# A decoder layer on one core: later closing of gates, other places for the attention values' products, earlier loads of the branches, and another order at the seam to the up-projection

## The chip, the cores and the metric

The kernel runs on one core of a Trainium2 chip. The time is that of the device, in microseconds, for one execution of the whole program. The engines are named as in the profile: PE multiplies matrices, ACT and DVE work on what lies in memory or in PE's accumulation banks, POOL works on memory only, SP issues transfers. Each engine works through its own queue in order and waits at an instruction until what that needs is there.

## The reference

One layer of a hybrid decoder, 1024 tokens of width 1024, all in float32:

```
h    = rms_norm(x);  P = h @ w_in                 # columns for all branches and their gates
y_a  = RWKV-7 mixing (8 heads x 64, state recurrence over the tokens, group norm)
y_b  = stick-breaking attention (8 heads x 64)
y_m  = cross-attention to 256 memory tokens (4 heads x 128)
merged = sum_b sigmoid(G_b) * (y_b @ w_branch[b])
x    = x + merged @ w_out
x    = x + (silu(gate) * val) @ w_down,  gate, val = conv3(rms_norm(x) @ w_up)
```

The result has to agree in float32. Most products are therefore done as three: each operand is split into a high half that PE takes at full rate and the rest, and high by high, high by low and low by high are summed.

## The kernel before, in words

Everything runs in one program whose order is written out by generators: an outer one (preparation of the recurrence, the two attentions, the recurrence itself) is woven with a filler, the projections and gates of later branches, which `yield` after each group of six matmuls. So a step of the outer work that is moved by one `yield` moves past one such group on PE (1.36 us, six matmuls), and instructions marked as pinned keep the order in which they were written on their engine. Within an engine nothing overtakes.

- **Preparation** (`rwkv_prep`, four head pairs). `shifted` takes a finished projection from its bank (L248), scales a shifted copy on ACT (L249) and adds both on DVE (L251). `chain` makes, per pair and half, the products bk (L381) and r times P (L382 to L384) from which `gram` multiplies on PE; `turned` has eight transposes and takes their result out of the bank on DVE at L398.
- **Stick-breaking attention** (`sb_attn`, 64 units). `front(u)` multiplies queries by keys and takes a sigmoid on ACT; `weigh(u)` is a scan on DVE (L838); `mid(u)` transposes the weights on PE and takes them out on ACT (L850); `back(u)` multiplies them by the values, for two units at a time, 32 times in all. The filler beside it are the gates of the branches (`gate_item`); a finished gate is closed by `close_gates` within the next gate (DVE L740, ACT L743, and a transfer).
- **Memory attention** (`mem_attn`, 8 units) has the same shape: scores, row maximum and Exp (DVE L1050, ACT L1053), transposes, values. Its queries come from `mem_q`, whose product is split at L1015 (ACT) and L1017 (DVE).
- **Recurrence and branches** (`stage2`, `branch`). The recurrence takes small products out of banks on ACT (L549, L561). For a branch `load_y` loads four tiles into buffers of tag `w4` and splits them: ACT L1101 for the high half, DVE L1102 for the low half. `norm_quarter` ends with a reciprocal root: `rsqrt` issues L168 on DVE and a power on POOL (L169), and L593 on DVE multiplies by it.
- **Output projection and seam** (`out_proj`, `up_phase`). Each of eight row tiles is multiplied, added to x (L1230), squared (L1231), normed (L1233, L168, L169, L1235), transposed (`spread`) and, as operand of a block scheme with seven products instead of eight, summed (L1261 to L1266) and split (L1271 on ACT, L1272 on DVE or POOL). In `up_phase` `prep1` to `prep3` provide the split weights (L1351, L1354) and `step(n, i)` issues product i of column pair n; L1448 takes the first product out of its bank.

The up and down products that follow run on PE from 1250 us to the end.

Of the kernel before, what the change touches and what calls it, by code (L numbers as in the profile page):

```python
# [49 lines left out]
class Trunk:  # L50
# [120 lines left out]
    def startup(self):  # L171
# [41 lines left out]
        self.wa = self.shifted(12, "A", pps[0])  # L213
        nc.scalar.activation(self.wa[0:64], self.wa[0:64], AF.Tanh)
        self.sg = self.shifted(13, "A", pps[1])
        nc.scalar.activation(self.sg, self.sg, AF.Sigmoid)
        return self.shifted(4, "at", pps[2])
# [24 lines left out]
    def shifted(self, ti, tag, pp=None):  # L242
# [7 lines left out]
        out = self.t4(tag)  # L250
        nc.vector.scalar_tensor_tensor(out, pr, self.omm[:, ti : ti + 1], tmp, ALU.mult, ALU.add)  # L251
        return out
# [35 lines left out]
    def shift_item(self, ti, out, name):  # L288
# [10 lines left out]
        out.append(self.shifted(ti, "at", pp))  # L299
        self.fresh.append(name)  # L300
        yield
# [5 lines left out]
    def rwkv_prep(self, p, krv, need):  # L307
# [66 lines left out]
        def chain(h):  # L374
            hs = halves[h]
            bk, ra = self.t4("qk"), self.t4("qk")
            bk4, ra4 = (x.rearrange("p (c u s) -> p c u s", c=8, u=2) for x in (bk, ra))
            for x, first in ((b, 1), (kp, 0)):
                for h2 in range(2):
                    q = slice(h2 * 64, h2 * 64 + 64)  # L380
                    nc.vector.tensor_tensor(bk4[q, :, first ^ h2], self.c8(x[q, hs]), self.c8(Q[q, hs]), ALU.mult)  # L381
            nc.vector.tensor_tensor(ra4[:, :, 0], self.c8(r[:, hs]), self.c8(P[:, hs]), ALU.mult)  # L382
            nc.vector.scalar_tensor_tensor(ra4[:, :, 1, 1:64], self.c8(P[:, hs])[:, :, 0:63], -1.0, self.c8(kk[:, hs])[:, :, 1:64], ALU.mult, ALU.mult)
            nc.vector.tensor_scalar(ra4[:, :, 1, 0], self.c8(kk[:, hs])[:, :, 0], -math.exp(OFF), None, ALU.mult)  # L384
# [188 lines left out]
    def norm_quarter(self, i, junk):  # L573
# [17 lines left out]
        yield  # L591
# [102 lines left out]
    def proj_item(self, src, fin, hook={}):  # L694
# [119 lines left out]
    def sb_attn(self, qk, need):  # L814
# [80 lines left out]
    def mem_kv(self):  # L895
# [18 lines left out]
        def ss():  # L914
            pst = self.ps("g")
            for j in range(2):
                for k in range(8):
                    o = (k % 4) * 256 + j * 128
                    self.colsum(pst[:, j : j + 1], sqs[k // 4][:, o : o + 128], self.ones[:, 0:1], k == 0, k == 7)
# [86 lines left out]
    def mem_q(self, h, out, hook):  # L1006
# [3 lines left out]
        def fin(pp):  # L1010
            sq = self.t4()
            qhi, qlo = self.t4("qk", F32R), self.t4("qk", F32R)
            for i in range(2):
                hs = slice(i * 512, (i + 1) * 512)
                nc.scalar.activation(qhi[:, hs], pp[i], AF.Copy, scale=self.par("memq"))  # L1015
                nc.scalar.activation(sq[:, hs], pp[i], AF.Square)
                nc.vector.scalar_tensor_tensor(qlo[:, hs], pp[i], self.par("memq"), qhi[:, hs].bitcast(F32), ALU.mult, ALU.subtract)  # L1017
# [11 lines left out]
    def mem_attn(self, mq, need):  # L1029
# [51 lines left out]
        for s in range(len(units) + 4):  # L1081
            if s >= 4:
                back(s - 4)
            if s < len(units):
                front(s)
            yield
            if 2 <= s < len(units) + 2:
                mid(s - 2)
# [56 lines left out]
    def branch(self, b, first):  # L1145
        st = {}

        def load():
            st["y"] = self.load_y(b)
# [6 lines left out]
        return load, items  # L1156
# [43 lines left out]
    def out_proj(self):  # L1200
# [21 lines left out]
        def norm(tt, pp):  # L1222
            x = self.t4()
# [4 lines left out]
            for n in range(2):  # L1228
                ns = slice(n * 512, (n + 1) * 512)
                nc.vector.tensor_tensor(x[:, ns], pp[n], x[:, ns], ALU.add)  # L1230
                nc.scalar.activation(sq[:, ns], x[:, ns], AF.Square, accum_out=ss[:, n : n + 1])  # L1231
            nc.scalar.dma_start(self.x2d[tt], x)
            nc.vector.tensor_tensor(rs, ss[:, 0:1], ss[:, 1:2], ALU.add)  # L1233
            self.rsqrt(rs, rs, 1, 1.0 / D, 1e-6)
            nc.scalar.activation(sq, x, AF.Copy, scale=rs)  # L1235
            return sq

        def spread(tt, sq):
            tl = slice((tt % 4) * 128, (tt % 4 + 1) * 128)
            for kb in range(2):  # L1240
# [4 lines left out]
                for kk in range(4):  # L1245
# [3 lines left out]
                    if kk < 2:  # L1249
                        nc.scalar.activation(dst, src, AF.Copy, scale=self.par("g2", k))  # L1250
# [604 lines left out]
```

## Time and profile before

| | |
|---|---|
| median of three runs | 1858.47 us (1855.64 to 1860.42) |
| the profiled execution, its own time | 1856.43 us |
| its span, first to last instruction | 1854.7 us |
| PE busy | 1796.9 us, 97% |
| DVE, ACT, POOL busy | 63%, 47%, 43% |
| mean granted clock of PE | 0.991 |

The span is what the rows of the trace add up to; the profiled execution's own time lies 1.73 us above it and the median 2.04 us above that. In rows of the timeline the columns are start, duration, engine, line, operation, operands, shape and count; in square brackets stands how long the engine idled just before and whom it waited for. A row of waits has the total, the number and the longest. In rows of windows each engine's busy time is followed by its number of instructions, and PEclk is the granted clock.

### The profile page before, as it was taken

What the parts mean: (1) busy time and instruction counts of PE and PEld (TensorE: products, weight loads), DVE (VectorE), ACT (ScalarE), POOL (GpSimd) and SP (SyncE); (2) the same over time, 40 slices, a digit from 0 to 9 for tenths busy, and PEclk for the clock granted to TensorE, in tenths of its full rate; (3) what the DMA queues carried; (4) which work ended last, traced back from release to release, by engine and by line L of the source; (5) the groups of instructions that cost most, each with busy time, mean ns of one, the idle gap of its engine ahead of it and who ended that gap; (6) DMA issues with size and microseconds to landing.
All of it is one profiled execution on the core that took longest, in us unless ns stands there. A gap on an engine that the chain in (4) does not pass through costs nothing. (4 is left out here: it accounts for less than half of the span.)

```text
span 1854.7 us, 27269 instructions
## 1 busy us (share of the span) xinstructions
PE 1796.9 (97%) x10468; PEld 1451.4 (78%) x10468; DVE 1170.1 (63%) x1623; ACT 866.7 (47%) x1553; POOL 788.6 (43%) x447
## 2 busy tenths in 40 slices
PE   8999999999999999998999999979999999999999
PEld 6777778778787887776777878768888888878877
DVE  5657664998887514334333882467776777785595
ACT  5443343565565635533443443454454444444433
POOL 2322343222221452122322541487776767545454
PEclk9999999999999999999999999999999999999999
DMA  4155465111112441568654462323232233395475
GB/s 180 58 170 182 158 201 187 49 43 64 40 52 78 112 128 40 177 237 281 229 171 161 163 235 102 114 68 109 95 124 88 97 114 108 120 326 203 141 247 185
DMA packets 122339, 261.28 MB, mean 141 GB/s; under 512 B 28505, under 2 KB 43097, under 8 KB 122082
## 3 DMA queue, kind: packets, MB, share of 16 engines
q1 hardware_dynamic: 84738, 193.71, 32.2%
q10 hardware_dynamic: 33696, 53.23, 7.9%
q0 software_dynamic: 3776, 12.62, 2.2%
q8 instruction: 82, 1.34, 0.3%
q14 instruction: 47, 0.39, 0.1%
HBM read 178.99 MB, written 80.48 MB: 140 GB/s over the span
## 5 line engine op out<-in xcount | busy, mean ns | idle before, releaser
L81 POOL TENSOR_TENSOR wl<-wr,wh 128x1024 fp32r<-128x1024 f32 x77 | 195.0, 2533 | 479.8 <-ACT wh L80 479.8
L112 PE MATMUL mm<-xhi,wh 128*128 128x512 f32 x784 | 266.0, 420 | 9.1 <-ACT xhi L182 7.4
L112 PE MATMUL mm<-xlo,wh 128*128 128x512 f32 x784 | 247.2, 397 | 0.7 <-DVE xlo L183 0.7
L112 PE MATMUL mm<-xhi,wl 128*128 128x512 f32 x784 | 244.4, 393 | 0.0
L112 PEld LDWEIGHTS mm<-xlo,wh 128*128 128x128 f32 x784 | 149.5, 191 | 35.1 <-DVE xlo L183 1.5
L112 PEld LDWEIGHTS mm<-xhi,wl 128*128 128x128 f32 x784 | 148.9, 190 | 33.8 <-POOL wl L81 0.5
L112 PEld LDWEIGHTS mm<-xhi,wh 128*128 128x128 f32 x784 | 138.5, 192 | 39.8 <-issue 9.1
L80 ACT ACTIVATE wh<-wr 128x1024 fp32r<-128x1024 f32 x77 | 81.5, 1059 | 153.8 <-PE mm L112 89.6
L112 PE MATMUL mm<-dw,da 128*128 128x512 f32 x528 | 121.3, 390 | 1.5 <-DVE da L1593 1.4
L112 PE MATMUL mm<-BT,l 128*128 128x512 f32 x504 | 117.9, 389 | 1.0 <-POOL l L1354 1.0
L112 PEld LDWEIGHTS mm<-dw,da 128*128 128x128 f32 x528 | 98.9, 188 | 23.3 <-DVE da L1593 2.3
L1594 POOL TENSOR_TENSOR dw<-draw,dw 128x512 fp32r<-128x512 f32 x55 | 80.5, 1471 | 84.9 <-ACT dw L1592 82.2
L112 PE MATMUL mm<-BT,wh 128*128 128x512 f32 x352 | 109.8, 393 | 3.2 <-DVE u L1406 3.2
L838 DVE TENSOR_TENSOR_SCAN at<-at,nrt 128x128 f32<-128x128 f32 (+3 forms) x64 | 91.2, 1428 | 32.3 <-ACT at L832 32.2
L112 PEld LDWEIGHTS mm<-BT,l 128*128 128x128 f32 x504 | 94.5, 188 | 21.0 <-POOL l L1354 1.4
L112 PE MATMUL mm<-B,wh 128*128 128x512 f32 x352 | 108.5, 389 | 2.1 <-ACT p L1448 2.1
L1593 DVE TENSOR_TENSOR da<-draw,da 128x512 fp32r<-128x512 f32 x77 | 67.0, 878 | 60.3 <-ACT da L1591 59.7
L112 PE MATMUL g<-dw,da 128*128 128x512 f32 x396 | 92.4, 394 | 2.2 <-ACT dw L1592 1.1
L1354 POOL TENSOR_TENSOR l<-it,l 128x1024 fp32r<-128x1024 f32 x21 | 50.8, 2421 | 94.4 <-ACT l L1351 94.4
L112 PEld LDWEIGHTS g<-dw,da 128*128 128x128 f32 x396 | 75.4, 191 | 18.7 <-ACT dw L1592 1.6
L1591 ACT ACTIVATE da<-draw 128x512 fp32r<-128x512 f32 x77 | 48.3, 629 | 84.3 <-PE mm L112 41.0
L169 POOL TENSOR_TENSOR hf<-rs,half 128x16 f32<-128x16 f32 (+1 forms) x17 | 48.5, 2856 | 86.1 <-DVE rs L168 85.7
(329 smaller groups left out, 3982.2 us busy)
## 6 DMA issues: line engine op xcount, KB each, us to landing
wr<-in_w_in_dram SPq DMA_DIRECT2D x50, 512.0 KB, 3.6
draw<-actd SPq DMA_DIRECT2D x77, 256.0 KB, 3.4
draw<-in_w_down_dram SPq DMA_DIRECT2D x55, 256.0 KB, 4.6
at<-scr SPq DMA_DIRECT2D x24, 512.0 KB, 6.2
wr<-in_w_up_dram SPq DMA_DIRECT2D x22, 512.0 KB, 3.5
actd<-gall ACTq DMA_DIRECT2D x44, 256.0 KB, 3.3
rw<-in_w_up_dram SPq DMA_DIRECT2D x20, 512.0 KB, 3.9
gsd<-w ACTq DMA_DIRECT2D x18, 512.0 KB, 2.7
```

The lines of the kernel that those rows point to most:

```text
L80: self.nc.scalar.activation(hi, raw, AF.Copy)
L81: self.nc.gpsimd.tensor_tensor(lo, raw, hi.bitcast(F32), ALU.subtract)
L112: self.pinned(self.nc.tensor.matmul(*a, **k))
L169: nc.gpsimd.tensor_tensor(out, t[:, :n], self.half[:, :n], ALU.pow)
L838: self.pinned(nc.vector.tensor_tensor_scan(sn[:, :W][:, ::-1], sn[:, :W][:, ::-1], self.nrt[:, 1152 - W :][:, ::-1], 1.0, ALU.mult, ALU.max))
L1354: nc.gpsimd.tensor_tensor(lo, src, hi.bitcast(F32), ALU.subtract)
L1591: self.pinned(nc.scalar.activation(A[:, 0], a, AF.Copy))
L1593: self.pinned(nc.vector.tensor_tensor(A[:, 1], a, A[:, 0].bitcast(F32), ALU.subtract))
L1594: nc.gpsimd.tensor_tensor(Wt[:, 1], w, Wt[:, 0].bitcast(F32), ALU.subtract)
```

## The change

It keeps the arithmetic and the number of matmuls and moves work:

- in the preparation r times P stands ahead of the bk products in `chain`; the last addition of `shifted` is issued one `yield` later; `turned(0)` comes one `yield` later and `gram(1, 0)` stays;
- in both attentions `front` comes first, then a `yield`, then `back`, directly ahead of the transposes of `mid`; gates are closed at the fifth group of the next gate instead of the third; `spread_last` is hooked into a gate;
- the two halves of the memory queries' split are pinned, and the norm sums of the memory keys are in two parts;
- a branch's y is loaded into the buffers of tag `A`, in which the low half then stays, and is split piece by piece in a gate that lies ahead of the branch;
- `norm_quarter` goes on three `yield`s after the root instead of one;
- in `out_proj` the four POOL splits of two operands are done two and two, the second two behind the norm of tile 4; in `up_phase` the norm of tile 7, the sums, the high and the low splits are written in another order, the first products have a bank each and are taken out at once, and the products of the first pair come in the order 5, 6, 7, 4, 3 instead of 6, 5, 7, 4, 3.

```diff
-        out.append(self.shifted(ti, "at", pp))
+        rest = self.shifted(ti, "at", pp)
+        yield
+        out.append(rest())
         self.fresh.append(name)
-        yield
...
         u1 = chain(1)
-        for _ in range(2):
+        for _ in range(3):
             yield
         turned(0, bp)
         bp = decayed(1, u1[0])
-        for _ in range(4):
+        for _ in range(3):
             yield
         gram(1, 0, *u1)
...
         self.rsqrt(rs, vs, 16, 1.0 / 64, 64e-5)
-        yield
+        for _ in range(3):
+            yield
...
-            if k == 2:
+            if k == 4:
                 self.close_gates()
...
         for u in range(len(units) + 4):
+            if u < len(units):
+                front(u)
             if u % 2 == 0:
+                yield
                 if u >= 4:
                     back(u - 4)
-                if u < len(units):
-                    front(u)
-                yield
-            elif u < len(units):
-                front(u)
             if 2 <= u < len(units) + 2:
                 mid(u - 2)
...
-                nc.vector.scalar_tensor_tensor(qlo[:, hs], pp[i], self.par("memq"), qhi[:, hs].bitcast(F32), ALU.mult, ALU.subtract)
+                self.pinned(nc.vector.scalar_tensor_tensor(qlo[:, hs], pp[i], self.par("memq"), qhi[:, hs].bitcast(F32), ALU.mult, ALU.subtract))
...
     def load_y(self, b):
-        ys = []
+        hi = self.pool_a.tile([128, 4, 1024], F32R, name=self.nm("yhi"), tag="inst")
+        los = [self.t4("A", F32R) for _ in range(4)]
         for k in range(4):
-            y = self.t4("w4")
-            self.nc.sync.dma_start(y, self.yd[b, k])
-            ys.append(y)
-        return self.split_y(ys)
+            self.nc.sync.dma_start(los[k].bitcast(F32), self.yd[b, k])
+
+        def part(k):
+            y = los[k].bitcast(F32)
+            self.pinned(self.nc.scalar.activation(hi[:, k], y, AF.Copy))
+            self.pinned(self.nc.vector.tensor_tensor(los[k], y, hi[:, k].bitcast(F32), ALU.subtract))
...
+        def side(i):
+            name, src = ("11", "21")[i], [halves(j)[i] for j in range(2)]
+            operand(name, self.pool_l, "l4")
+            split_hi(name, src)
+            split_lo(name, src, nc.gpsimd)
...
+            drain(norm(tt, pp))
+            if tt == 4:
+                side(1)
...
+        hi("22", old)
+        hi("T1", old, (0,))
+        hi("T2", old)
+        next(norm)
+        lo("T1", old, (0,))
+        next(norm)
+        hi("T1", old, (1,))
+        lo("T2", old)
+        lo("22", old, eng=nc.gpsimd)
         step(0, 1)
-        step(1, 1)
-        late(7)
...
+        evacuate(0)
+        next(norm, None)
+        st[1, "A"] = bank()
+        product(1, 1, st[1, "A"], True, True)
+        spread()
+        evacuate(1)
...
-        items += [lambda: drain(inv), ld1, gate(), gate(), mark("y1"), *br1, ld2, gate(), *br2, gate()]
+        items += [lambda: drain(inv), gate(), ld1, gate(hk1), mark("y1"), *br1, ld2, gate(hk2), *br2, gate()]
```

**ACT, the load of branch 2 within the recurrence**, before (w is the tile that y was loaded into, yhi the high half, qk the recurrence's matrices taken out of banks g):

```order
L80 ACTIVATE wh_7571<-wr_7569 128x1024
L1101 ACTIVATE yhi_7556<-w_1310_7548 128x1024
L549 ACTIVATE qk_7234<-g_7469 64x64 x2
L549 ACTIVATE qk_7234<-g_7470 64x64
L1101 ACTIVATE yhi_7556<-w_1311_7550 128x1024
L549 ACTIVATE qk_7234<-g_7470 64x64
L549 ACTIVATE qk_7239<-g_7471 64x64 x2
L549 ACTIVATE qk_7239<-g_7472 64x64 x2
L561 ACTIVATE qk_6779<-g_7469 64x64 x2
```

and now (L1121 is the former L1101, L554 the former L549, L566 the former L561):

```order
L80 ACTIVATE wh_7555<-wr_7553 128x1024
L554 ACTIVATE qk_7230<-g_7465 64x64 x2
L554 ACTIVATE qk_7230<-g_7466 64x64 x2
L554 ACTIVATE qk_7235<-g_7467 64x64 x2
L554 ACTIVATE qk_7235<-g_7468 64x64 x2
L1121 ACTIVATE yhi_7544<-A_7545 128x1024
L1121 ACTIVATE yhi_7544<-A_7546 128x1024
L566 ACTIVATE qk_6764<-g_7465 64x64 x2
```

The splits no longer stand within the eight L549 but behind them, and ahead of the eight L561.

**POOL, output projection**, before (B are the low halves of two operands, ss the root of tile 4's norm):

```order
L1272 TENSOR_TENSOR B_1_1_10238<-raw_9862,B_0_1_10236 128x1024
L1272 TENSOR_TENSOR B_1_0_10245<-raw_9862,B_0_0_10243 128x1024
L1272 TENSOR_TENSOR B_1_1_10246<-raw_9862,B_0_1_10244 128x1024
L169 TENSOR_TENSOR ss_1616_10272<-rs_10279,half 128x1
L1303 TENSOR_TENSOR wsum_10352<-wsec_10351 128x512
```

and now:

```order
L1292 TENSOR_TENSOR B_1_1_10230<-raw_9854,B_0_1_10228 128x1024
L169 TENSOR_TENSOR ss_1608_10256<-rs_10263,half 128x1
L1292 TENSOR_TENSOR B_1_0_10269<-raw_9854,B_0_0_10267 128x1024
L1292 TENSOR_TENSOR B_1_1_10270<-raw_9854,B_0_1_10268 128x1024
L1327 TENSOR_TENSOR wsum_10344<-wsec_10343 128x512
```

Two of the four splits have gone behind the root.

**ACT, the seam**, before (p takes the first product out of its bank, sq is tile 7's norm, BT and B high halves):

```order
L1231 ACTIVATE sq_10549,ss_1646_10551<-w_1645_10548 128x512 x2
L1235 ACTIVATE sq_10549<-w_1645_10548,ss_1646_10551 128x1024
L1271 ACTIVATE BT_0_0_10567<-t_1575_9867 128x2x384
L1271 ACTIVATE B_0_0_10579<-A_9865 128x2x384
L1271 ACTIVATE BT_0_1_10568<-t_1576_9868 128x2x384
L1271 ACTIVATE B_0_1_10580<-A_9866 128x2x384
L1448 ACTIVATE p_1649_10605<-mm_10592 128x512
L1448 ACTIVATE p_1651_10620<-mm_10607 128x512
```

and now:

```order
L1244 ACTIVATE sq_10568,ss_1638_10570<-x_1637_10567 128x512 x2
L1287 ACTIVATE BT_0_1_10550<-raw_9854 128x2x384
L1473 ACTIVATE p_1641_10599<-mm_10586 128x512
L1250 ACTIVATE sq_10568<-x_1637_10567,ss_1638_10570 128x1024
L1265 ACTIVATE A_9855<-g_10615,params 128x128 x2
L1265 ACTIVATE A_9857<-g_10624,params 128x128 x2
L1473 ACTIVATE p_1645_10633<-mm_10602 128x512
```

The first product is taken out ahead of the norm's last step, and the splits that stood between have gone ahead of the squares.

More of the change, by code (lines that the diff above doesn't have):

```diff
@@ L1086, in mem_attn @@
             yield
+            if s >= 4:
+                back(s - 4)
             if 2 <= s < len(units) + 2:
@@ L1268, in split @@
-        def split(name, src, eng, ts=slice(0, 512)):
-            for j in range(2):
+            sub = lambda o, x, y: self.pinned(nc.vector.tensor_tensor(o, x, y, ALU.subtract))
+            for half in which:
+                for j in range(2):
+                    b11, b21, b12, b22 = (x[:, :, ts] for x in halves(j))
+                    if half == 0:
+                        sub(b11, b12, b11)
+                        sub(t2[j][:, :, ts], b22, b11)
+                    else:
+                        sub(b12, b22, b12)
+                        sub(b21, t2[j][:, :, ts], b21)
@@ L1311, in out_proj @@
         w1 = weights(0, "at")
+        drain = lambda g: [None for _ in g]
         for tt in range(2):
-            sqs[tt] = norm(tt, first[tt])
+            drain(norm(tt, first[tt]))
         for tt in range(2, 8):
@@ L1499, in u1_first @@
             nc.scalar.activation(u[:, L2], A, AF.Copy)
-        def parts(name, eng):
-            for ts in (old, new):
-                split(name, src[name], eng, ts)
+        hi = lambda name, ts=slice(0, 512), js=(0, 1): split_hi(name, src[name], ts, js)
+        lo = lambda name, ts=slice(0, 512), js=(0, 1), eng=nc.vector: split_lo(name, src[name], eng, ts, js)
         self.pin = True
```

160 lines of the change are left out of this document (90 added, 70 removed).

## The prediction

> **What bounds the kernel now.** I read the page first, then the chain of waits, the waits of PE, and around each of them the timeline of the engine that PE waited for.
>
> ```profile
> PE 1796.9 (97%) x10468; PEld 1451.4 (78%) x10468; DVE 1170.1 (63%) x1623; ACT 866.7 (47%) x1553; POOL 788.6 (43%) x447
> 1250.28 381.40 PE mm L112 x1680
> 1250.00:1640.00 390.00, 389.72 (x1718) 322.40 (x1719) 292.37 (x438) 182.70 (x252) 271.19 (x158) 1.00 0.34 113
> ```
>
> PE is the bound: in the long up phase the chain is one piece of 1680 matmuls, and 1718 in 390 us make 0.227 us each. The change adds no matmul, and whatever is saved ahead of 1250 us moves all that follows. At most 1854.7 - 1796.9 = 57.8 us of idle PE can be won, plus lost clock.
>
> ```profile
> PE g L105 <- DVE at L398: 6.4, 3, 2.6
> PE g L112 <- ACT qk L549: 6.0, 1, 6.0
> PE g L105 <- ACT at L850: 3.7, 2, 2.8
> PE g L112 <- ACT at L1053: 2.8, 1, 2.8
> 1226.50:1229.90 3.40, 3.40 (x10) 2.64 (x9) 0.00 (x0) 0.21 (x2) 3.32 (x4) 0.50 0.00 0
> 1230.00:1233.40 3.40, 3.40 (x17) 2.77 (x16) 1.92 (x3) 2.49 (x3) 3.40 (x3) 1.00 0.39 106
> ```
>
> The idle is a few single waits. The last two rows show a second loss: 3.4 us at half clock after an idle, with 10 matmuls where the next 3.4 us hold 17. Half of 3.4 us, 1.7 us, is lost each time. By the granted clock in such rows, the idles at 103, 496, 718, 873 (two windows), 985 and 1171 us are followed by such a window; those at 217 and 272 are not.
>
> **The change, part by part.** *Preparation.*
>
> ```profile
> 103.52 1.92 PE L105 MATMUL g<-kon,it 128*128 128x128 f32 x8 [2.23 <-DVE at L398]
> 216.63 1.16 PE L105 MATMUL g<-kon,it 128*128 128x128 f32 x8 [1.62 <-DVE at L398]
> 272.25 1.25 PE L105 MATMUL g<-kon,it 128*128 128x128 f32 x8 [2.57 <-DVE at L398]
> 101.48 1.28 DVE L251 SCALAR_TENSOR_TENSOR at<-w,omm,w 128x1024 f32<-128x1024 f32 x1 [1.21 <-ACT w L249]
> 102.69 2.48 DVE L398 TENSOR_TENSOR at<-g,kon 128x512 f32<-128x512 f32 x4
> 153.47 1.16 PE L112 MATMUL g<-qk,qk 64*128 64x128 f32 x16 [1.68 <-DVE qk L384]
> 153.24 2.79 DVE L381 TENSOR_TENSOR qk<-qk,qk 64x512 f32<-64x512 f32 x4
> ```
>
> The transposes wait for banks that L398 empties; L398 stands behind L251, which waits 1.21 us for ACT and takes 1.28. Now L251 is issued one group later, behind L398, and the transposes too come 1.36 us later: 1.21 + 1.28 + 1.36 = 3.85 us, more than the longest of the three waits. They go: 2.23 + 1.62 + 2.57 and one window of 1.7, 8.1 us. Against it, the grams at 153 and 208 need the last bk product, which now ends the row of products on DVE where the short L384 did: one of four L381, 0.70 us, each. That makes 6.7.
>
> *Stick-breaking attention.*
>
> ```profile
> 495.99 1.07 PE L105 MATMUL g<-kon,at 128*128 128x128 f32 x4 [2.78 <-ACT at L850]
> 494.39 1.06 ACT L743 ACTIVATE w<-w 128x1024 f32<-128x1024 f32 x1 [4.99 <-DVE w L740]
> sum 300.00, PE 291.79 PEld 237.40 DVE 252.57 ACT 171.25 POOL 77.48; mean PE 48.63 PEld 39.57 DVE 42.09 ACT 28.54 POOL 12.91
> ```
>
> ACT stood 4.99 us at the closing of a gate, with L850 behind it. Closed two groups later (2.7 us and the attention's work between them), the closing finds L740 done: 2.78 + 1.7 = 4.5. For the values' products themselves I take nothing: the same matmuls are issued, their operands two units old. What their new neighbours cost is bounded, either way, by 32 x 0.12 = 3.8 us: the pair of matmuls at 1209.70 (below), first of its kind after others, takes 0.73 where a pair in a row takes 0.61. DVE is busy 252.57 of 300 us here (the sum of six windows from 300 to 600 us), so waits for it can form anew; I take 3.0 off.
>
> *Memory attention.*
>
> ```profile
> 718.45 2.93 PE L112 MATMUL g<-A,qk 128*128 128x256 f32 x12 [2.77 <-ACT at L1053]
> 715.22 0.75 DVE L1017 SCALAR_TENSOR_TENSOR qk<-mm,params,qk 128x512 fp32r<-128x512 f32 x1 [3.02 <-ACT w L1016]
> 716.95 0.22 DVE L1050 SCALAR_TENSOR_TENSOR nb<-mxt,hf 128x2 f32<-128x2 f32 x2
> 739.73 1.98 PE L112 MATMUL mm<-at,A 128*128 128x512 f32 x4 [1.19 <-DVE qk L1017]
> ```
>
> The short L1050 that Exp waits for stood behind two L1017, the first of which waited 3.02 us. With both pinned it stands ahead, 4.5 us sooner (3.02 + 2 x 0.75): 2.77 + 1.7. At 739.73 the values now come a front and a group later, more than 1.19 us. In all 5.7.
>
> *Recurrence and branches.*
>
> ```profile
> 873.08 0.95 PE L112 MATMUL g<-it,at 64*64 64x64 f32 x8 [6.04 <-ACT qk L549]
> 866.21 0.69 ACT L549 ACTIVATE qk<-g 64x64 f32<-64x64 f32 x3
> 871.73 1.06 ACT L1101 ACTIVATE yhi<-w 128x1024 fp32r<-128x1024 f32 x1 [4.83 <-DMA w<-yd]
> w<-yd SPq DMA_DIRECT2D x3, 512.0 KB, 5.6
> 863.48 0.61 PE L112 MATMUL mm<-A,wh 128*128 128x512 f32 x2
> 985.08 1.28 PE L112 MATMUL g<-it,at 64*64 64x64 f32 x12 [0.98 <-ACT qk L561]
> 982.06 1.10 DVE L593 TENSOR_TENSOR qk<-qk,hf 128x256 f32<-128x256 f32 x3 [3.04 <-POOL hf L169]
> ```
>
> A split waited 4.83 us for its load and held five of eight L549 back. Now the eight stand ahead: 6.04 and two windows, 9.4. But the loads into tag `A` wait until PE has read branch 1 out of it, 863.48 + 0.61 = 864.1; 5.6 us of landing make 869.7, two splits of 1.06 end at 871.8, and the next evacuations (L561, eight in 1.90) at 873.7, while PE without the stall would want them near 871.5: a rest of 0 to 2.2 us, 1.4 taken. SP's queue is held by these loads until 864; what lies behind it is wanted from 880. Root at 985: two groups more, 2.7 us, ahead of L593 leave 0.3 of its 3.04 wait, so 0.98 + 1.7 go. Together 8.0 + 2.7 = 10.7.
>
> *Output projection and seam.*
>
> ```profile
> 1170.93 1.09 PE L105 MATMUL g<-kon,w 128*128 128x128 f32 x8 [2.08 <-ACT w L1235]
> 1159.73 9.47 POOL L1272 TENSOR_TENSOR B<-raw,B 128x1024 fp32r<-128x1024 f32 x4 [6.38 <-ACT B L1271]
> 1190.00:1250.00 60.00, 50.96 (x218) 39.98 (x216) 37.92 (x71) 33.16 (x59) 43.15 (x24) 0.97 0.29 97
> 1206.55 1.03 PE L105 MATMUL g<-kon,sq 128*128 128x128 f32 x8
> 1209.70 0.73 PE L112 MATMUL mm<-B,wh 128*128 128x512 f32 x2 [2.12 <-ACT p L1448]
> 1209.07 1.06 ACT L1448 ACTIVATE p<-mm 128x512 f32<-128x512 f32 x2
> 1210.03 1.13 ACT L1250 ACTIVATE A<-g,params 128x128 f32<-128x128 f32 x4
> 1216.02 9.84 POOL L1354 TENSOR_TENSOR wl<-wsec,wh 128x1024 fp32r<-128x1024 f32 x1 [2.09 <-ACT wh L1351]
> 1234.51 2.39 POOL L1354 TENSOR_TENSOR l<-it,l 128x1024 fp32r<-128x1024 f32 x1
> 1236.96 5.28 PE L112 MATMUL mm<-BT,l 128*128 128x512 f32 x22 [0.96 <-POOL l L1354]
> ```
>
> The root stood behind 9.47 us of splits; two of four fewer bring it 4.7 us forward: 2.08 + 1.7 = 3.8. At 1209.70 the evacuation now precedes the splits, and 2.12 goes; but POOL decides what that is worth. PE's second pair started with the end of `l` at 1236.90, last of a row without gaps from wl at 1216.02. Tile 7's evacuations (L1250), which waited for L1448 to end at 1210.03, can run from about 1207.1, when the first four of the eight transposes (1206.55, 1.03) are done, 2.9 us sooner, and wl's source with them; `l` now stands ahead of another split of 2.4. So 5.3, bounded by nothing (wl still crowded, a new wait for it in the third product) and by all idle of the stage, 60 - 50.96 = 9.0, and 1.7 of clock.
>
> That wl took 9.84 us where the same shape takes 2.4 decides this bound: DVE was splitting from memory all the time. [...] I go by the 9.84. [...]
>
> **The sum**: 6.7 + 4.5 + 5.7 + 10.7 + 3.8 + 5.3 = 36.7. Off it 3.0 for DVE, and 2.0 for clock windows: about 20 idles of 0.9 us or more had 8 or 9 windows behind them, so of eight that stay three, not two as now, may draw one. Net 31.7, of the profiled execution 1856.43 - 31.7 = 1824.7; the median lay 2.04 higher: **1827 us**.
>
> **Rivals.** *DVE takes over*: preparation and attention give nothing, since each wait that goes turns up again behind DVE's 84%. For it: the 64 scans there; against: only 6.4 us of PE's waits name L398. 1827 + 6.7 + 4.5 = 1838.
>
> *The clock windows are not tied to these idles*: six of the seven windows counted as won (all but one pair's first at 873) come back elsewhere, 10.2 us less the 2.0 allowed: 1835. For it: 1.62 and 2.57 us of idle drew none and 0.98 did. [...]
>
> *Slower*: `back` directly ahead of `mid` takes the bank turn that the transposes wanted, and each of 32 steps waits for an evacuation as the two waits on L850 did. It decides from 1 us a step; at the 1.19 of the values' wait at 739.73, the nearest in kind, 32 x 1.19 = 38 against 31.7 gives 1858.5 + 6 = 1865. Against: L850 was waited for twice in 64.
>
> *It does not do what it says*: waits are replaced one for one, PE idles as before, 1857.
>
> **How the numbers follow.** Forecast 0.58 (own range 1818 to 1836), DVE 0.18, clock 0.12, no effect 0.06, slower 0.06. Faster than by 0.3% (5.6 us, about what can be told from no change) are the first three: 0.88; the same 0.05, slower 0.07, as the rivals shade into each other. The range: below, all of the seam's bound (5.4 more), the rest of 1.4 and the allowances of 5 make 1815, with the grams' 1.4 1814, and some 2 for waits not credited; above, DVE and clock together, 1827 + 11.2 + 8.2 = 1846, and to 1848.
>
> **What would show it.** In the profile after: no wait of PE on L398's successor, none of 6 us in the recurrence and no stretch at half clock there; the seam's first product taken out ahead of the norm's last step, without PE waiting; PE's second pair starting as `l` ends. Wrong would be: waits of PE on the scans or on L850 that were not there, DVE above 90% from 300 to 600 us, or a first split of branch 2 that waits for its load with L561 behind it for more than 2 us.

## The result, and the profile after

The changed kernel takes 1831.95 us (median; 1831.08 to 1832.8), the kernel before, timed beside it, 1858.26. The ratio is 0.9859, with an interval from 0.9842 to 0.9876: 26.3 us less. The forecast was 1827 us, 31.5 less than the median known then. So the sign and most of the size came out, and 5 us are missing. As the experiments show, the terms of the sum fared much less well than their total.

First the page's row of busy time of the changed kernel, then the longest of its waits of PE behind the 7.4 us for the first operand at the start, which both kernels have.

```profile
PE 1788.1 (98%) x10468; PEld 1445.7 (79%) x10468; DVE 1174.4 (64%) x1622; ACT 865.8 (47%) x1553; POOL 786.2 (43%) x447
```

```profile
PE g L105 <- ACT at L856: 4.3, 4, 2.6
PE g L112 <- ACT qk L566: 2.2, 2, 1.4
PE mm L112 <- POOL wl L81: 2.1, 1, 2.1
PE g L105 <- DVE at L844: 2.1, 1, 2.1
```

The span fell from 1854.7 to 1829.7 us. PE's busy time gave 8.8 of these 25.0: the same 10468 matmuls, but four stretches of 3.4 us at half clock inside the program where there were ten. Part of that is chance: a second profile of the kernel before (`b_ctl`) has seven, one of the changed kernel (`a_ctl`) three. Its idle time gave 16.2: 57.8 before, 1829.7 - 1788.1 = 41.6 after. The wait of 6.0 us in the recurrence and the 2.8 of the memory attention are off the list. Of the three waits on L398 (now L403) one is left, shown below, and those on L850 (now L856) are four instead of two.

To see where the time went, both spans are cut into six stretches that hold the same work to within nine matmuls: up to 300 us the preparation, then stick-breaking attention, memory attention, recurrence and the first branches, the rest up to the seam, and (without a row here) the up phase to the end. The rows of windows of the kernel before:

```profile
0.00:300.00 300.00, 282.27 (x1534) 217.85 (x1535) 183.66 (x216) 130.14 (x158) 94.55 (x46) 0.99 0.51 167
300.00:600.00 300.00, 291.79 (x1965) 237.40 (x1964) 252.57 (x242) 171.25 (x307) 77.48 (x33) 0.99 0.18 58
600.00:860.00 260.00, 255.71 (x1804) 207.40 (x1803) 92.72 (x180) 127.16 (x281) 81.17 (x56) 0.99 0.48 149
860.00:1000.00 140.00, 132.40 (x1342) 103.36 (x1340) 58.01 (x148) 60.57 (x197) 40.88 (x22) 0.96 0.59 202
1000.00:1250.00 250.00, 238.10 (x1215) 193.73 (x1214) 144.44 (x236) 107.58 (x210) 120.06 (x63) 0.99 0.42 144
```

and of the changed kernel, cut about where the same matmuls now stand:

```profile
0.00:298.00 298.00, 282.62 (x1543) 219.02 (x1544) 184.04 (x218) 131.46 (x159) 95.75 (x46) 0.99 0.52 171
298.00:595.00 297.00, 288.78 (x1957) 235.61 (x1956) 251.56 (x241) 167.93 (x302) 78.30 (x33) 0.99 0.18 56
595.00:848.00 253.00, 252.65 (x1798) 204.97 (x1797) 94.23 (x176) 127.91 (x285) 81.70 (x55) 1.00 0.48 153
848.00:982.00 134.00, 130.65 (x1341) 101.92 (x1340) 59.72 (x152) 59.10 (x194) 41.42 (x22) 0.99 0.60 207
982.00:1226.00 244.00, 236.76 (x1221) 192.30 (x1220) 146.05 (x235) 109.37 (x212) 112.20 (x61) 1.00 0.43 148
```

The first number behind the bounds is the length of a stretch, the second PE's busy time. The lengths fell by 2, 3, 7, 6, 6 and 1 us (the last from 1854.7 - 1250 to 1829.7 - 1226). The prediction's terms for the first five are 6.7, 1.5 (4.5 less 3.0 for DVE), 5.7, 10.7 and 9.1, with 2.0 off for the clock. Nearly all that was idle in the third went (260 - 255.71 = 4.3 us before, 253 - 252.65 = 0.35 after); by these cuts the first and the fourth fell short most, by 4.7 each, and the fifth by 3.1. With up to nine matmuls more or fewer in a stretch that is good to about 2 us; the table further down goes by single matmuls. DVE is at 251.56 of 297 us in the second, 85%, as before.

**Three waits that should have gone and stayed.** The rows of the timeline of the changed kernel around 213 us:

```profile
211.30 1.28 DVE L253 SCALAR_TENSOR_TENSOR at<-w,omm,w 128x1024 f32<-128x1024 f32 x1 [1.21 <-ACT w L249]
212.50 2.48 DVE L403 TENSOR_TENSOR at<-g,kon 128x512 f32<-128x512 f32 x4
213.33 1.16 PE L105 MATMUL g<-kon,it 128*128 128x128 f32 x8 [2.06 <-DVE at L403]
```

The shift's last instruction (L253) with its 1.21 us of waiting still stands ahead of L403, and PE waits 2.06 us where it waited 1.62. Around 493 us:

```profile
491.90 1.06 ACT L749 ACTIVATE w<-w 128x1024 f32<-128x1024 f32 x1 [5.07 <-DVE w L746]
492.86 0.58 ACT L856 ACTIVATE at<-g 128x512 f32<-128x512 f32 x1
493.49 0.66 PE L105 MATMUL g<-kon,at 128*128 128x128 f32 x4 [2.55 <-ACT at L856]
```

The closing of a gate (L749) stands on ACT ahead of the same evacuation (L856) as before, and idles 5.07 us there, before 4.99. And around 968 us:

```profile
965.61 1.10 DVE L599 TENSOR_TENSOR qk<-qk,hf 128x256 f32<-128x256 f32 x3 [3.04 <-POOL hf L169]
967.82 0.85 DVE L564 SCALAR_TENSOR_TENSOR it<-it,pc,g 128x64 f32<-128x64 f32 x4
968.63 1.28 PE L112 MATMUL g<-it,at 64*64 64x64 f32 x12 [1.38 <-ACT qk L566]
```

The multiplications behind the root (L599) wait the same 3.04 us to the hundredth, with the recurrence's L564 behind them. Two groups of delay were put ahead of them in the program, and they stand where they stood.

**One new wait.** The first matmul that wants a low part of a weight at 259 us, on PE and on POOL:

```profile
254.54 1.90 POOL L415 TENSOR_TENSOR it<-qk,pc 128x1024 f32<-128x1024 f32 x1 [8.71 <-DVE qk L389]
256.40 6.10 POOL L81 TENSOR_TENSOR wl<-wr,wh 128x1024 fp32r<-128x1024 f32 x2
259.25 0.50 PE L112 MATMUL mm<-wl,xhi 128*128 128x512 f32 x1 [2.09 <-POOL wl L81]
```

POOL stood 8.71 us for a bk product, which DVE now makes last, and the weight's splits (L81) queued behind it. Before, PE came to this place at 261.77 us, 4.6 us later than it now would without the wait, just as the split ended (258.88 + 2.84 = 261.72). POOL now ends it only 2.5 us sooner.

**What came as predicted.** The second branch's loads and the seam:

```profile
857.94 1.06 ACT L1121 ACTIVATE yhi<-A 128x1024 fp32r<-128x1024 f32 x1 [1.45 <-DMA A<-yd]
859.19 1.06 ACT L1121 ACTIVATE yhi<-A 128x1024 fp32r<-128x1024 f32 x1 [0.18 <-DMA A<-yd]
861.20 1.87 ACT L566 ACTIVATE qk<-g 64x64 f32<-64x64 f32 x8 [0.95 <-DVE it L564]
861.70 1.28 PE L112 MATMUL g<-it,at 64*64 64x64 f32 x12 [0.80 <-ACT qk L566]
...
1186.79 0.58 ACT L1473 ACTIVATE p<-mm 128x512 f32<-128x512 f32 x1
1187.91 1.15 ACT L1250 ACTIVATE sq<-x,ss 128x1024 f32<-128x1024 f32 x1 [0.54 <-POOL ss L169]
...
1194.73 2.97 DVE L1292 TENSOR_TENSOR BT<-t,BT 128x256 fp32r<-128x256 f32 x2
1194.98 2.43 POOL L1382 TENSOR_TENSOR wl<-wsec,wh 128x1024 fp32r<-128x1024 f32 x1 [3.18 <-ACT wh L1379]
...
1210.76 2.36 POOL L1382 TENSOR_TENSOR l<-it,l 128x1024 fp32r<-128x1024 f32 x1
```

The two splits wait 1.45 and 0.18 us for their loads, and of 6.04 us PE waits 0.80 (predicted: 0 to 2.2). The seam's first product (L1473) is taken out ahead of the norm's last step (L1250), and PE's second pair starts, after 1.6 us of waiting, as `l` ends (L1382, 1210.76 + 2.36 = 1213.1).

### The profile page after: what moved, and what is told of

It reads as the page before. It is cut to its first block, busy times and chain, and to the rows that moved or that the text cites. A ratio compares the mean times of both kernels' runs of the same rounds, so it can differ in the third digit from the quotient of the medians.

```text
span 1829.7 us, 27286 instructions
## 1 busy us (share of the span) xinstructions
PE 1788.1 (98%) x10468; PEld 1445.7 (79%) x10468; DVE 1174.4 (64%) x1622; ACT 865.8 (47%) x1553; POOL 786.2 (43%) x447
## 4 chain that ended last, share of the span: by engine, by line
PE 65%; DVE 7%; issue 4%; POOL 3%; ACT 2%; DMA 2%; SPq 0%; POOLq 0%; ACTq 0%; DVEq 0%
PE mm L112 53%; PE g L112 10%; PE g L105 3%; DVE it L469 1%; POOL dw L1653 1%; DVE inst L471 1%; DVE at L844 1%; DVE qk L807 1%; DMA wr<-in_w_out_dram 1%; DVE mg L1211 0%; DVE w L746 0%; DVE at L1204 0%; POOL wl L81 0%; DVE at L1203 0%; DVE qk L791 0%
## 5 line engine op out<-in xcount | busy, mean ns | idle before, releaser
L81 POOL TENSOR_TENSOR wl<-wr,wh 128x1024 fp32r<-128x1024 f32 x77 | 195.2, 2537 | 510.2 <-ACT wh L80 492.4
L1382 POOL TENSOR_TENSOR l<-it,l 128x1024 fp32r<-128x1024 f32 x21 | 50.8, 2419 | 92.1 <-ACT l L1379 92.1
L746 DVE TENSOR_TENSOR w<-w,nrt 128x1024 f32<-128x1024 f32 x24 | 46.8, 1949 | 56.1 <-ACT w L745 52.9
```

The costliest lines, as they stand in the source:

```text
L81: self.nc.gpsimd.tensor_tensor(lo, raw, hi.bitcast(F32), ALU.subtract)
L746: nc.vector.tensor_tensor(g, g, self.nrb, ALU.mult)
L1382: nc.gpsimd.tensor_tensor(lo, src, hi.bitcast(F32), ALU.subtract)
```

## The experiments

Two questions are open. Which part of the change gave what: the prediction's terms, with nothing for the values' place, against any other split of the same total. And why three waits stayed. The theory for that: the order of the program binds only where instructions are pinned, and the scheduler left the moved but unpinned pieces where they had been. Its rival: the pieces moved, and something else, DVE or a late operand, holds PE at the same place.

### Each part alone

Five kernels are the kernel before with one part of the change each. `p_prep` has the later half of the shift, the other order of the products and the two numbers of groups in the preparation:

```diff
-        out.append(self.shifted(ti, "at", pp))
+        rest = self.shifted(ti, "at", pp)
+        yield
+        out.append(rest())
...
-        for _ in range(2):
+        for _ in range(3):
             yield
         turned(0, bp)
...
```

> The kernel before with the changes of the preparation alone (shifted, chain, turned and gram). By the trace of the changed kernel only the wait at 103 us with its half-clock window goes, the one at 217 us stays and the one at 272 us turns into a wait for POOL's wl: about 4 us less than before (2 to 5), with a wait of PE on L403 of about 2 us left. By the prediction's term 6.7 us less and no wait on L403.

Measured: 1858.09 us, ratio 0.9986 (0.9965 to 1.0007), 2.6 us of 1859 with an interval from -1.3 to 6.5, so no gain is shown by the times. In its trace the wait at 103 us is gone; PE waits 2.11 at 212.66 and 2.18 for the weight's split at 258.71, as in the full change.

`p_attn` has only the places of the values' products in both attentions:

```diff
+            if u < len(units):
+                front(u)
             if u % 2 == 0:
+                yield
                 if u >= 4:
                     back(u - 4)
-                if u < len(units):
-                    front(u)
-                yield
-            elif u < len(units):
-                front(u)
             if 2 <= u < len(units) + 2:
                 mid(u - 2)
...
```

> The kernel before with the values' products moved directly ahead of the transposes in both attentions, nothing else. Theory: the place of the products is worth nothing by itself, 0 us (-2 to +2), and the 2.8 us wait on L850's row near 496 us stays. Rival 1: the place carries the gain of the attentions, 4 to 8 us less, with that wait gone. Rival 2: it costs a bank turn in each of 32 steps, over 10 us more.

Measured: 1852.49 us, ratio 0.9967 (0.9953 to 0.9981), 6.1 us (3.5 to 8.7). This goes against the prediction, which took nothing for the step, and against the theory for this run; the size is that of its first rival, though the wait near 496 us went only in part. The row of lines of the kernel before from 300 to 660 us (instructions, busy time, mean of one, idle time ahead of them with its releasers), for the transposes:

```profile
L105 PE MATMUL g<-kon,at 128*128 128x128 f32 x288 | 43.3, 275 | 6.4 <-ACT at L850 3.7 <-DVE at L838 1.6 <-DVE hn L685 1.1
```

and of `p_attn`:

```profile
L105 PE MATMUL g<-kon,at 128*128 128x128 f32 x288 | 44.9, 280 | 4.1 <-ACT at L850 2.9 <-DVE hn L685 1.0 <-ACT at L832 0.2
```

The transposes wait 4.1 us instead of 6.4: the 1.56 on the scan (L838) is gone and the 2.78 on L850 is 1.53. A plausible reason, which no run isolates, is that the values' matmuls now give ACT and DVE their own duration in which to empty the banks that the transposes want. The 1.19 of the values' wait at 739.73 is gone too. By the position of the same matmuls in the two traces this kernel is 7.3 us ahead of the kernel before at 750 us. Of these, 2.3 arose ahead of 300 us, where the two programs are the same (`b_ctl` is 2.0 ahead there as well), so 5.1 belong to the step. It then loses about 5 at the seam; the last section comes back to that.

`p_branch` has the loads and splits of the branches and the two more groups ahead of the root's multiplications:

```diff
+            hooks.update({3 + k: parts[k] for k in range(4)})
...
+        items += [lambda: drain(inv), gate(), ld1, gate(hk1), mark("y1"), *br1, ld2, gate(hk2), *br2, gate()]
...
-        yield
+        for _ in range(3):
+            yield
```

> The kernel before with the new loads and splits of the branches and the longer pause behind the root, nothing else. Theory: the 6.04 us wait near 873 us goes with its two half-clock windows, a rest of about 0.8 us comes in its place, and the 1 us wait behind the root near 985 us stays: 7 to 9 us less. By the prediction's term 10.7 us less with the wait behind the root gone.

Measured: 1851.67 us, ratio 0.9965 (0.9948 to 0.9983), 6.5 us (3.2 to 9.7). In the trace the wait of 6.04 us is 0.74, and the matmuls, 0.3 us ahead up to there, stand 5.6 ahead once the half-clock stretches of both kernels are over (from 884 us); one such stretch still follows the 0.74 here. The wait on the root is there (1.35 at 980.5). Of the lead 2.8 us are lost between 1070 and 1100 us and 5 more at the seam.

`p_seam` has the output projection and the seam:

```diff
-            nc.scalar.activation(sq, x, AF.Copy, scale=rs)
-            return sq
+            yield
+            self.pinned(nc.scalar.activation(sq, x, AF.Copy, scale=rs))
+            sqs[tt] = sq
```

> The kernel before with the changes of output projection and seam alone. Theory, which is also the prediction's: 2.1 us and a window at 1171 us partly go (2.3 to 3.8) and POOL's row ahead of the second pair ends 5 to 6 us sooner: 7 to 10 us less. Rival: as POOL's wl is still crowded by DVE's splits, PE waits for it in the third product and the seam gives under 4 us.

Measured: 1849.05 us, ratio 0.9946 (0.9931 to 0.996), 10.0 us (7.4 to 12.8), where the prediction's terms were 3.8 + 5.3 = 9.1. In its trace the matmuls gain 3.9 us on the kernel before at 1171 us and 4.4 between 1200 and 1245 us.

`p_mem` has what is left: the pinned splits and the sums in two halves in the memory attention, the closing two groups later, and the spreading as a hook of the first gate:

```diff
-            if k == 2:
+            if k == 4:
                 self.close_gates()
...
+                self.pinned(nc.scalar.activation(qhi[:, hs], pp[i], AF.Copy, scale=self.par("memq")))
...
+            items += [... gate({6: self.spread_last} if p == 0 else {}), kss, qp, gate(hooks), mark(f"sb{p}")]
```

> The kernel before with the memory branch's changes (the pins of the queries' split, the norm sums in two parts), the later closing of gates and the hooked spread_last, nothing else. Theory: the pins alone clear the 2.77 us wait near 718 us with its half-clock window and 1.2 us near 740 us, and the closing adds nothing: 3 to 6 us less than before. By the prediction's two terms, 4.5 + 5.7, it would be 10 us less.

Measured: 1857.58 us, ratio 0.9996 (0.9979 to 1.0013), 0.7 us (-2.4 to 3.9), below the 3 to 6 expected for this run. Of its waits of PE:

```profile
PE g L105 <- ACT at L850: 4.3, 2, 3.8
```

The wait of 2.77 us at 718 is gone, as predicted, and there the matmuls gain 4.1 us. But the 1.19 near 740 us is still there, against the theory for this run; the wait behind the closing is 3.8 instead of 2.78 us, the scan's is 2.1 instead of 1.56, and POOL's split is waited for 1.38 at 661.5. This run doesn't separate which of its edits brought these; what the later closing does by itself is measured by `e_k2` below.

Together the five make 2.6 + 6.1 + 6.5 + 10.0 + 0.7 = 25.9 us, against 26.3 for the whole. That agreement says little about each one: the profiled executions of three of them lose some 5 us in the old seam, which the full change does not have, and how often the kernel before loses them is not known.

### The changed kernel with one edit

The changed kernel was run again beside these as `a_ctl`.

> The changed kernel once more, as the measure for the three runs beside it on the same chip: 1830 to 1834 us.

Measured: 1829.7 us (1828.97 to 1831.12), ratio 0.9846 (0.983 to 0.9863), just below the range expected.

`e_k2` closes the gates where the kernel before did:

```diff
-            if k == 4:
+            if k == 2:
                 self.close_gates()
```

> The changed kernel, gates closed at the third group again instead of the fifth. Theory: the closing's Sigmoid is not held to its place in the program and stands at nearly the same place on ACT, so the edit is worth nothing: 0 us against the changed kernel (-2 to +1.5), the wait on L856 near 493 us between 1.5 and 2.6. The prediction's term: the later closing carries 4.5 us, so 4.5 more without it.

Measured: 1831.0 us, ratio 0.9854 (0.9835 to 0.9874); no difference from `a_ctl`. Its waits on L856 are the same:

```profile
PE g L105 <- ACT at L856: 4.1, 3, 2.6
```

and so is the closing's place, ahead of the evacuation that PE waits for:

```profile
490.02 1.06 ACT L749 ACTIVATE w<-w 128x1024 f32<-128x1024 f32 x1 [5.10 <-DVE w L746]
```

`e_sig` makes the place binding instead: the Sigmoid of the closing is pinned.

```diff
-                nc.scalar.activation(g, g, AF.Sigmoid, scale=-1.0)
+                self.pinned(nc.scalar.activation(g, g, AF.Sigmoid, scale=-1.0))
```

> The changed kernel with the closing's Sigmoid held to its place in the program, so that closing at the fifth group does move it on ACT. Theory: the wait of 2.55 us on L856 near 493 us goes, 1 to 4 us less than the changed kernel. Rival: the wait moves on to another evacuation or to the gates' buffers that come free later: 0, or slower.

Measured: 1826.06 us (1824.61 to 1828.26), ratio 0.9827 (0.9809 to 0.9845), 3.6 us less than `a_ctl`. The timeline of ACT at the place that is at 492 us in the changed kernel:

```profile
486.77 1.09 ACT L856 ACTIVATE at<-g 128x512 f32<-128x512 f32 x2
487.75 1.06 ACT L749 ACTIVATE w<-w 128x1024 f32<-128x1024 f32 x1
```

The evacuations stand ahead, the closing finds its operand ready, and no wait on L856 is left in the whole kernel; there were four with 4.3 us. With `e_k2` this settles the step: the number in the program did not move the instruction, and with the pin it moved. Whether the pin would do as much at the third group is not shown.

`e_root` pins the multiplications behind the root:

```diff
-            nc.vector.tensor_tensor(g3(y), g3(y), b3(rs, p), ALU.mult)
+            self.pinned(nc.vector.tensor_tensor(g3(y), g3(y), b3(rs, p), ALU.mult))
```

> The changed kernel with the multiplications behind the root (L599) held to their place in the program, three yields behind it. Theory: DVE then has the recurrence's L564 ahead of them, L566 runs in time and the wait of 1.38 us near 969 us goes, with the half-clock window behind it: 1.4 to 3.1 us less than the changed kernel. Rival: DVE is late with the recurrence for another reason, and nothing changes.

Measured: 1826.12 us (1824.66 to 1830.36), ratio 0.9824 (0.9804 to 0.9843), 3.6 us less by the medians, with ranges that overlap at the end: one of the four times, 1830.36, is no better than `a_ctl`. The timeline at the place that is at 968 us in the changed kernel:

```profile
963.44 0.84 DVE L564 SCALAR_TENSOR_TENSOR it<-it,pc,g 128x64 f32<-128x64 f32 x4
963.75 1.87 ACT L566 ACTIVATE qk<-g 64x64 f32<-64x64 f32 x8 [2.07 <-DVE it L564]
966.94 0.57 PE L112 MATMUL g<-it,at 64*64 64x64 f32 x12
```

L564 no longer stands behind the wait for the root, and PE does not wait. This is the trace of that slowest execution. From 980 to 990 us on its matmuls gain 3.2 us on those of the kernel before, where those of `a_ctl` gain 0.6 and those of the changed kernel's first profile lose 1.0; 2.5 of it are lost again by 1100 us, and a half-clock stretch follows at 1211 us, where `a_ctl` has none.

`e_two` has both pins, and `e_three` also issues the first transposes of the preparation one group later:

```diff
-        for _ in range(3):
+        for _ in range(4):
             yield
         turned(0, bp)
         bp = decayed(1, u1[0])
-        for _ in range(3):
+        for _ in range(2):
             yield
```

> The changed kernel with both held to their places: the closing's Sigmoid and the multiplications behind the root. Theory: they act at different places and add, 6 to 8 us less than the changed kernel, 1822 to 1824 us. Rival: half-clock windows come back at other idles and half of it is left, 1826.

> As the one before, and turned(0) of the preparation one group of matmuls later still. Theory: the wait of 2.1 us on L403 near 213 us shrinks by the 1.36 us of a group, about 1.4 us less than the one before. Rival: L403 is bound by what stands ahead of it on DVE and the transposes only delay the gram behind them: 0.

Measured: `e_two` 1821.08 us, ratio 0.9789 (0.9773 to 0.9805); `e_three` 1817.07 us (1814.59 to 1823.2), ratio 0.9776 (0.9753 to 0.9798). The two pins add up: 8.6 us below `a_ctl` by the medians, 10.6 by the ratios (0.0057 of 1858), against 3.6 + 3.6; 6 to 8 were expected. What the later transposes add lies inside the intervals, but their row in `e_three` is clear:

```profile
212.89 1.16 PE L105 MATMUL g<-kon,it 128*128 128x128 f32 x8 [0.75 <-DVE at L403]
```

The wait at 213 us is 0.75 instead of 2.06, and this execution has no half-clock stretch inside the program. `e_three` is the fastest of these versions, 41.7 us (0.0224 of 1859.47) below the kernel before. Against the profiled changed kernel its span is 12.9 us shorter: 7.6 of PE's busy time (now 1780.5), which is mostly clock, and 5.3 of idle. New waits took part of the gain back. They are in its waits of PE:

```profile
PE g L105 <- ACT sq L1250: 3.1, 1, 3.1
...
PE mm L112 <- DVE at L1203: 2.3, 3, 1.2
```

The waits on L856 and L566 and most of L403's, 4.3 + 2.2 + 1.3 = 7.8 us, went, and of that 2.4 came back at the seam's norm (0.7 in the changed kernel) and 1.6 at L1203 (0.7 in the changed kernel).

`b_ctl` is the kernel before once more, for its profile.

> The kernel before once more, for a second profile of its seam: if DVE and POOL can meet there in two ways, PE's wait behind L1406 is about 7 us and POOL's wl about 2.4 us, as in the three profiles with one other part changed; if the first profile is the rule, 2.5 us and 9.8 us.

Measured: 1854.6 us. Its seam is used in the last section.

## Why the prediction was right, and where it was wrong

The sign, the bound by PE and the range held, and none of the four rivals came in. DVE did not take over (85% in the attention; the one wait on a scan is 2.1 instead of 1.56 us). Half-clock stretches became fewer together with the idles. `back` ahead of `mid` did not cost a bank turn; alone it gained. But two of the prediction's signs of being right failed: a wait of 2.06 us on L398's successor is left, and a stretch at half clock still stands at 970.8 us in the recurrence. And one of its signs of being wrong showed: PE waits for L850's successor four times (4.3 us) where it waited twice (3.7).

How far the same matmuls of the changed kernel's profile are ahead of those of the kernel before shows what each stretch gave. The limits are those of the kernel before; `b_ctl`, the same program, drifts by about 2 us against the first profile, so each row is good to no more than that.

| stretch, us | gained, us | term, us |
|---|---|---|
| 0 to 300, preparation | 3.9 | 6.7 |
| 300 to 690, stick-breaking | 1.2 | 4.5 - 3.0 |
| 690 to 750, memory | 5.6 | 5.7 |
| 750 to 900, loads of the branch | 6.8 | 8.0 |
| 900 to 1000, root | -1.0 | 2.7 |
| 1000 to 1160 | -0.8 | 0 |
| 1160 to 1200, output projection | 2.6 | 3.8 |
| 1200 to 1250, seam | 5.5 | 5.3 |
| 1250 to the end | 1.2 | 0 |

- **Recurrence and branches, 10.7.** The mechanism of the loads was right, with a rest of 0.74 to 0.80 us in the range 0 to 2.2. Its size was too high: 6.8 us here, 5.3 alone and 5.2 in `a_ctl`, which both still have a half-clock stretch behind the rest. One reason is in the profile of before: the two half-clock stretches behind the 6.04 us began at 871.5 us, so 1.5 us of them fell into the idle itself and cost nothing. The 2.7 of the root were wrong: "two groups more ahead of L593" did not happen on DVE. The same 3.04 us wait stood in the same place, and with a pin `e_root` gains 3.2 us there in its trace.
- **Stick-breaking, 4.5.** The step "closed two groups later, the closing finds L740 done" failed for the same reason: the closing is not pinned, and its place on ACT did not change. With and without the later number the time is the same; with a pin the term comes, 3.6 us.
- **The values' place, 0.** Mis-sized: 6.1 us alone (3.5 to 8.7). I had looked for its cost in the neighbours of matmuls, and bounded it either way by 3.8, but not asked what PE's work on the values covers when it stands ahead of an instruction that waits. Within the whole change it can't be seen as such: there the stretch gave 1.2 us, with 4.3 us of waits on the transposes' evacuations where `p_attn` has 2.9.
- **Preparation, 6.7.** Mis-sized; alone it gave 2.6 (-1.3 to 6.5). Of three waits the first went. At 217 "issued one group later, behind L398" is true of the program but not of DVE, where L253 still stood ahead of L403; no run pins L253, so that the scheduler put it back is argued here, and not shown as for the other two. The wait at 272 went, but PE, being earlier, came to the split of a weight at 259 before it was ready: 2.09 us. The bk product, which I had priced by the grams that need it, holds POOL as well, and the weight's split is queued behind it; that this order made POOL late is read from the rows, no run isolates it. The 1.4 taken off for the grams did not come: they wait 2.1 us for bk, before 2.3.
- **Memory, 5.7.** Right: both waits are gone, and the place gave 5.6. The 1.19 at 739 belongs to the values' place, as the parts show: it is gone in `p_attn` and still there in `p_mem`. In `p_mem` the place gave 4.1, and new waits at 345, 498 and 661 took it away again.
- **Output projection and seam, 9.1.** Right in sum: 10.0 alone by the times, 8.3 in that kernel's trace, 8.1 here. The root's wait in the output projection went wholly in `p_seam`; in the whole change 1.02 of its 2.08 us are left. That POOL decides the seam, and PE's second pair starts as `l` ends, is what the rows show. The worry about wl was not borne out in its form: wl took 2.43 us, not 9.84, and what ran beside POOL on DVE took longer: 2.97 for two short splits, then 3.56 and 3.44 where the kernel before has 2.48 and 2.34. Nor did the 7.4 us that wl took less (9.84 - 2.43) lift the seam to its upper bound, since PE still waits for `l`, at the end of POOL's row.
- **Allowances, 5.0.** DVE's 3.0 were spent on little (0.5 at the scan). The clock's 2.0 were about right: in the profiles there are six half-clock stretches fewer, where seven were counted as won, though that number varies by chance (last section).

So the nearness of the total, 26.3 for 31.5, is partly luck: the root and the preparation fell 6.5 short together, the loads and the output projection 2.4, the closing's 4.5 did not come at all, and against that stood DVE's 3.0, hardly used, the clock's 2.0, and 1.2 that the stick-breaking stretch gave without the closing.

## What to carry to other kernels

A number of groups, or a line moved in the program, is not a place on an engine: for every term that rests on "now stands behind", look at that engine's own order after the change, instruction by instruction, and where a scheduler is free to put it back, pin it or count nothing. Price a move of work also by the time it covers in its new place, not only by its own duration. A stall that goes brings the engine earlier to everything behind it, so look for the next operand that was ready by just that margin, and for what is queued behind its producer.

## What the runs showed of the hardware

**The half-clock stretches of these traces lie on a grid.** In the changed kernel the idle of 1.38 us at 968 is followed by a stretch at half clock (PEclk 0.50, ten matmuls in 3.3 us):

```profile
967.20:970.60 3.40, 1.59 (x31) 1.13 (x32) 3.40 (x8) 1.75 (x8) 2.34 (x1) 1.00 0.00 0
970.80:974.10 3.30, 3.30 (x10) 2.59 (x9) 0.39 (x3) 0.00 (x0) 0.49 (x1) 0.50 0.42 164
```

In the profiled execution of `a_ctl`, the same kernel, the same idle (1.35 us at 970.43) is followed by none, and one stands behind the idle of 0.78 us in the recurrence at 861.90, which drew none in the other execution:

```profile
864.60:867.80 3.20, 3.20 (x9) 2.42 (x9) 2.10 (x2) 0.00 (x0) 0.00 (x0) 0.50 0.92 325
```

And `e_three` has none inside the program though it has idles of 3.1 and 2.2 us. Part of this can be read from the clock records of the profiles before and after. Each of their half-clock stretches inside the program lasts 3.413 us (at 871.54 two follow each other, 6.827 in all), and within a profile their starts lie whole multiples of that apart; in the kernel before, the one at 103.54 and the next at 154.74 are 51.20 = 15 x 3.413 apart. I divided the two profiles into slots of 3.413 us on that grid, from the first clock record at 14.8 and 14.9 us to the last matmul, and summed, slot by slot, PE's idle time, the time in which no matmul's record runs. All nine slots with 1.95 us of idle or more are followed by a slot at half clock; of the 14 with 1.2 to 1.95 us, five are; of the 1044 with less, none. So in these two profiles an idle counted by how it fell on the grid. If the slots of `e_three` lie as these two rows do, its 3.1 us, which end at 1176.58, fall into two of them (3.40 - 2.08 = 1.3 us and 3.40 - 1.62 = 1.8):

```profile
1171.40:1174.80 3.40, 2.08 (x10) 1.38 (x8) 3.20 (x6) 2.52 (x6) 0.58 (x1) 1.00 0.36 147
1174.80:1178.20 3.40, 1.62 (x11) 1.50 (x12) 1.27 (x3) 2.11 (x6) 3.40 (x3) 1.00 0.05 19
```

The slot at 967.20 above has 1.8 us of idle. What decides below 1.95 us stays open; the 3.4 us ahead of the stretch at 864.60 have 1.2 us as well. How many stretches there are thus differs from one execution of a kernel to the next: the kernel before has ten and seven, the changed kernel four and three. Removing idles still went with fewer: ten, four and none, at 57.8, 41.6 and 36.3 us of idle PE.

**The old seam has more than one outcome.** With the same instructions in the seam, DVE's splits and POOL's meet differently from one execution to another. In the profile of before, POOL's wl took 9.84 us while DVE's splits ran at 2.49, 2.48 and 2.34 us. In `p_attn`, whose seam is the old one, the timeline of POOL and DVE reads:

```profile
1210.50 2.45 POOL L1352 TENSOR_TENSOR wl<-wsec,wh 128x1024 fp32r<-128x1024 f32 x1 [2.09 <-ACT wh L1349]
...
1216.90 1.61 POOL L1368 TENSOR_TENSOR it<-wr 128x512 f32<-128x512 f32 x1 [3.96 <-DMA wr<-in_w_up_dram]
...
1221.29 2.25 POOL L1381 TENSOR_TENSOR s<-wr,it 128x512 f32<-128x512 f32 x1
```

```profile
1215.56 4.65 DVE L1270 TENSOR_TENSOR BT<-A,BT 128x768 fp32r<-128x768 f32 x4
1220.13 4.49 DVE L1270 TENSOR_TENSOR BT<-raw,BT 128x1024 fp32r<-128x1024 f32 x2
...
1225.27 1.22 PE L112 MATMUL mm<-BT,wh 128*128 128x512 f32 x2 [7.13 <-DVE u L1404]
```

Here wl took 2.45 us, DVE's splits nearly twice their time, POOL's short ones up to 2.25 instead of 1.29, and PE stood 7.13 us behind DVE where it stood 2.48. `p_prep` and `p_branch` have such a wait as well (8.2 and 7.1 us): each of the three was ahead before the seam and lost 5 to 6 us there. `p_mem` has 2.5, as the kernel before. `b_ctl` shows a third form, neither of the two expected of it: wl 2.44, DVE's first two short splits 2.94 where they took 0.75 and its long ones 2.48, 2.48 and 2.35, one POOL instruction of 4.69 where it took 1.27, PE's wait 2.83. What decides which form comes, no run shows. The change of form may be part of why the times of the kernel before spread over some 14 us (1851.8 to 1865.6), and those of the changed kernel over 4. It is not all of it: `p_seam`, which does not have the old seam, spreads over 7.5 us and `e_three` over 8.6.
